# Gate and up of seven groups: heads and rests of the tokens in one product of 512 columns

## The chip, the cores and the metric

The kernel runs on one NeuronCore of a Trainium2 chip. Its time is the device time of one execution in microseconds; runs are told by their median. Profiles and traces are of one profiled execution each, from the hardware profiler.

## The reference

A decoder trunk of two layers for one sequence of 512 tokens with 1,024 features, all in float32. Layer 0 mixes tokens by causal pooling, layer 1 by dilated window attention. Each mixer is followed by a SwiGLU feed-forward layer with 2,816 inner features; each of the four blocks is added to its input behind an RMS norm, and a last norm ends the trunk.

```python
D_FF = -(-8 * D_MODEL // (3 * 256)) * 256          # 2816

def swiglu(h, w_gate, w_up, w_down):
    g = jnp.einsum('bsd,df->bsf', h, w_gate)
    u = jnp.einsum('bsd,df->bsf', h, w_up)
    return jnp.einsum('bsf,fd->bsd', jax.nn.silu(g) * u, w_down)
...
    for i in range(DEPTH):
        h = rmsnorm(x, norm_mix[i])
        ...                                        # y = pool_mixer or attn_mixer of h
        x = x + y
        h = rmsnorm(x, norm_ffn[i])
        x = x + swiglu(h, w_gate[i], w_up[i], w_down[i])
    return rmsnorm(x, norm_final)
```

## The kernel before, in words

**Heads and rests.** The operands of TensorE (PE) are in float32r, a rounded 32-bit type. To keep float32 accuracy, each operand is held as a head ("hi", the value rounded) and a rest ("lo", what rounding took away), and each product is three matmuls into one sum: whi·hi, whi·lo and wlo·hi. A matmul loads a weight block of 128 x 128 and streams 256 or 512 columns through it.

**Weights.** The function `weights` hands out the weights of the next product. They are listed in one queue in the order of use (`enqueue_ffn`); transfers on the queue of SyncE (SP) fill buffers `wraw` and `vraw`, and for sums of two weight blocks a second transfer on GpSimd's queue (POOL) adds the second block while it lands, or VectorE (DVE) adds two buffers (L145). ScalarE (ACT) casts to the head `whi` (L139), DVE subtracts for the rest `wlo` (L143). Both are made up to four products ahead of the one in work.

**Gate and up.** The 2,816 inner features are 22 tiles of 128; a group is two of these, with their gate and up weights, so there are 11 groups. `Group` computes a group's gate and up sums for all tokens as a product of 2 x 2 blocks (feature tile by half of the 1,024 inputs, times that half by half of the tokens) with seven block products instead of eight. Its products i = 0 to 6 go into three PSUM sums: p takes 0, 2, 4 and 6, r takes 1 and 5, q takes 3. Each product (L625) runs over gate and up (g) and four chunks of 128 inputs (c), three matmuls of 256 columns each: 24 matmuls. Its weights are sums or differences of blocks, and its right operand, `RIGHT[i]`, one of seven token blocks: four lie in the normed tokens `h_hi` and `h_lo`, three are differences, in `t_hi` and `t_lo`.

Between the products, `Group.done` moves partial sums on. ACT copies p to `keep` behind product 0 (L636), r to a quarter of `ct` behind product 1 (L638), p to another behind product 2 (L640). DVE adds or subtracts behind products 3 to 5 (L642 to L646). Behind products 5 and 6 ACT applies Silu to the gate quarters (L647, L649, L653), DVE multiplies by up, and `first_half` and `second_half` combine the quarters into the seven left operands `u` of the down product, again as heads and rests (L320 ACT, L321 DVE).

**Down.** For blocks of three groups, `down` does the product with w_down by the same scheme of seven, 18 matmuls of 512 columns for each of two token blocks of 128 x 2 (L712), and DVE adds or subtracts each sum to the residual stream `x` (L719, L721).

**Order.** PE runs in the order in which the program is written: groups 0 and 1 interleaved, groups 2 and 3, down of block 0, groups 4 to 6, down of block 1, groups 7 to 9, down of block 2, group 10, and a last down product for groups 9 and 10 without the scheme. For the other engines a scheduler sorts by priority when the program is built, and the order of an engine's instructions is fixed by then. What runs right behind a product has priority `URGENT`. The kernel uses eight PSUM banks of 512 columns: four are `mm`, and p and r have two buffers each in the feed-forward layer.

## Time and profile before

| | |
|---|---|
| median of three runs | 1000.8 us (1000.61 to 1001.02) |
| the profiled execution | 1000.84 us, span of its instructions 999.0 us |
| granted clock of TensorE | 0.999 |
| busy PE / DVE / ACT / POOL | 990.7 / 784.6 / 529.5 / 113.1 us |
| matmuls | 6575 |
| the chain: gate and up (L625: p, r, mm) | 25%, 13% and 6% of the span |
| the chain: down (L712: r, p, mm) | 10%, 5% and 2% of the span |

The chain of waits follows the work that ended last back from the end: what released each instruction, or the one before it on its engine. Its rows give a start, a length and a name, with the count of instructions that were merged. Rows of groups give line, engine, operation, tile names (out<-in) and shape, then busy time and mean duration in ns, then the engine's idle time ahead of them and what ended it. A matmul's duration reaches into those behind it, so its price in a stream is the distance between starts. A row of windows gives the stretch, its length, then for PE, weight loads, DVE, ACT and POOL the busy time and number of instructions, then the clock and the transfers.

### The profile page before, as it was taken

How to read it: one execution, taken by the hardware profiler on the slowest of the kernel's cores; microseconds unless marked ns; L12 is line 12 of the kernel's file. 1: busy time of each engine (PE TensorE's matmuls, PEld its weight loads, DVE VectorE, ACT ScalarE, POOL GpSimd, SP SyncE). 2: the span in 40 equal slices, each digit the busy share in tenths (PEclk: the TensorE clock that was granted, in tenths of full speed). 3: DMA queues.
4: the chain of work that ended last, by engine and by line, in shares of the span. 5: the costliest groups of instructions: out<-in, count | busy, mean ns of one | idle time of the engine just before them, and what ended most of it. 6: DMA issues, size and time to landing. Idle time of an engine off the chain costs nothing.

```text
span 999.0 us, 16591 instructions
## 1 busy us (share of the span) xinstructions
PE 990.7 (99%) x6575; PEld 908.5 (91%) x6575; DVE 784.6 (79%) x1116; ACT 529.5 (53%) x838; POOL 113.1 (11%) x114
## 2 busy tenths in 40 slices
PE   9999999999999999999999999999999999999997
PEld 8888999989989998989888899899998998999896
DVE  6475799898888888777887557479989889788875
ACT  5573666545644554573543544356654554455354
POOL 0002010110011100002112024101011100111000
PEclk9999999999999999999999999999999999999999
DMA  9457277668559755524211249427666855975522
GB/s 334 177 168 190 60 197 177 151 187 233 149 126 292 182 137 148 183 76 135 83 58 53 62 153 284 92 64 196 174 158 200 234 148 123 289 179 138 155 67 84
DMA packets 76461, 157.29 MB, mean 157 GB/s; under 512 B 5904, under 2 KB 6288, under 8 KB 76384
## 3 DMA queue, kind: packets, MB, share of 16 engines
q1 hardware_dynamic: 58000, 121.00, 36.2%
q0 software_dynamic: 18096, 34.98, 20.3%
q8 instruction: 51, 0.84, 0.3%
q10 hardware_dynamic: 288, 0.27, 0.1%
q14 instruction: 26, 0.21, 0.1%
HBM read 154.08 MB, written 2.13 MB: 156 GB/s over the span
## 4 chain that ended last, share of the span: by engine, by line
PE 97%; ACT 1%; DMA 1%; DVE 1%; POOL 0%; issue 0%; DVEq 0%; ACTq 0%
PE p L625 25%; PE r L625 13%; PE r L712 10%; PE mm L625 6%; PE p L712 5%; PE mm L766 4%; PE mm L227 4%; PE mm L229 4%; PE mm L228 4%; PE mm L712 2%; PE early L443 2%; PE mm L363 2%; PE mm L361 2%; PE mm L362 2%; PE early L490 1%; PE tp L955 1%
## 5 line engine op out<-in xcount | busy, mean ns | idle before, releaser
L139 ACT CAST whi<-wraw 128x1024 fp32r<-128x1024 f32 (+2 forms) x189 | 184.9, 981 | 186.7 <-issue 45.8
L143 DVE TENSOR_TENSOR wlo<-wraw,whi 128x1024 fp32r<-128x1024 f32 (+2 forms) x190 | 221.1, 1165 | 76.2 <-ACT whi L139 75.7
L139 ACT CAST whi<-vraw 128x1024 fp32r<-128x1024 f32 (+1 forms) x102 | 99.6, 977 | 144.8 <-DVE vraw L145 53.7
L625 PE MATMUL p<-t_hi,wlo 128*128 128x256 f32 x528 | 149.8, 284 | 0.0
L625 PE MATMUL p<-t_lo,whi 128*128 128x256 f32 x528 | 149.4, 283 | 0.0
L625 PE MATMUL p<-t_hi,whi 128*128 128x256 f32 x528 | 148.4, 281 | 0.0
L143 DVE TENSOR_TENSOR wlo<-vraw,whi 128x1024 fp32r<-128x1024 f32 (+1 forms) x102 | 114.9, 1127 | 14.0 <-ACT whi L139 13.7
L625 PEld LDWEIGHTS p<-t_hi,whi 128*128 128x128 f32 x528 | 100.0, 189 | 0.0
L625 PE MATMUL r<-h_hi,wlo 128*128 128x256 f32 x352 | 99.9, 284 | 0.0
L625 PEld LDWEIGHTS p<-t_hi,wlo 128*128 128x128 f32 x528 | 99.6, 189 | 0.0
L625 PE MATMUL r<-h_lo,whi 128*128 128x256 f32 x352 | 99.6, 283 | 0.0
L625 PEld LDWEIGHTS p<-t_lo,whi 128*128 128x128 f32 x528 | 99.3, 188 | 0.0
L625 PE MATMUL r<-h_hi,whi 128*128 128x256 f32 x352 | 99.0, 281 | 0.0
L145 DVE TENSOR_TENSOR vraw<-vraw,wraw 128x1024 f32<-128x1024 f32 x68 | 76.6, 1127 | 0.8
L107 POOL DMA_DIRECT2D wraw<-w x22 | 26.7, 1211 | 435.6 <-DVE wlo L143 125.5
L625 PEld LDWEIGHTS r<-h_hi,whi 128*128 128x128 f32 x352 | 66.7, 189 | 0.0
L625 PEld LDWEIGHTS r<-h_hi,wlo 128*128 128x128 f32 x352 | 66.4, 189 | 0.0
L625 PEld LDWEIGHTS r<-h_lo,whi 128*128 128x128 f32 x352 | 66.2, 188 | 0.0
L227 PE MATMUL mm<-h_hi,whi 128*128 128x512 f32 (+1 forms) x176 | 64.8, 368 | 0.0
L229 PE MATMUL mm<-h_hi,wlo 128*128 128x512 f32 (+1 forms) x176 | 63.6, 361 | 0.0
L228 PE MATMUL mm<-h_lo,whi 128*128 128x512 f32 (+1 forms) x176 | 63.5, 361 | 0.0
L712 PE MATMUL r<-whi,u_lo 128*128 128x512 f32 x144 | 56.1, 390 | 0.0
(329 smaller groups left out, 2493.8 us busy)
## 6 DMA issues: line engine op xcount, KB each, us to landing
wraw<-w SPq DMA_DIRECT2D x116, 512.0 KB, 4.7
wraw<-w_down SPq DMA_DIRECT2D x32, 512.0 KB, 3.6
vraw<-w SPq DMA_DIRECT2D x22, 512.0 KB, 5.2
wraw<-w POOLq DMA_DIRECT2D x22, 512.0 KB, 7.6
vraw<-w POOLq DMA_DIRECT2D x22, 512.0 KB, 8.6
wraw<-wT SPq DMA_DIRECT2D x16, 512.0 KB, 4.4
wraw<-w_down SPq DMA_DIRECT2D x24, 256.0 KB, 2.7
vraw<-w_down SPq DMA_DIRECT2D x6, 512.0 KB, 5.5
```

Source lines behind the costliest of these rows:

```text
L107: nc.gpsimd.dma_start(dst, more, accum_op=ALU.add)
L139: nc.scalar.copy(hi[:, :n], raw[:, :n])
L143: nc.vector.tensor_sub(lo[:, :n], raw[:, :n], hi[:, :n].bitcast(F32))
L145: nc.vector.tensor_add(raws[into][:, :n], raws[into][:, :n], raws[more][:, :n])
L227: nc.tensor.matmul(ps, lhsT=whi, rhs=xhi, start=first, stop=False, **kw)
L228: nc.tensor.matmul(ps, lhsT=whi, rhs=xlo, start=False, stop=False, **kw)
L229: nc.tensor.matmul(ps, lhsT=wlo, rhs=xhi, start=False, stop=last, **kw)
L361: nc.tensor.matmul(ps, lhsT=xhi, rhs=w[0][:, k, :], start=first, stop=False)
L362: nc.tensor.matmul(ps, lhsT=xhi, rhs=w[1][:, k, :], start=False, stop=False)
L625: nc.tensor.matmul(ps[:, g, :], lhsT=w[:, g, c, :], rhs=xx[:, c, :], start=i in (0, 1, 3) and g + c + k == 0, stop=c == 3 and k == 2, skip ...
L712: nc.tensor.matmul(acc[t], lhsT=u, rhs=w, start=i in (0, 1, 3) and c + k == 0, stop=c == len(pairs) - 1 and k == 2, skip_group_check=True,)
L766: nc.tensor.matmul(ps, lhsT=u, rhs=w[:, m, :], start=z + m + k == 0, stop=z == 1 and m == 1 and k == 2,)
```

## The change

Groups 3 to 9 ("paired") of each layer get another form of product. The other groups keep theirs.

- Heads and rests of the tokens become one tile (`h`, `t2` to `t4`), so that one matmul can stream both: 256 columns of hi and 256 of lo.
- A paired group's sums are two banks for each of gate and up: four tiles of two banks, two called A (used by turns), one Q and one C, which take all eight. `mm` is closed and opened again around these groups.
- Products 0, 2, 3, 5 and 6 stream hi and lo through whi in one matmul of 512 columns, so that whi·hi and whi·lo lie side by side, and wlo·hi is added to one of the two halves. Products 1 and 4 keep three matmuls of 256.
- 0, 2, 4 and 6 go to A, 3 to Q, 1 and 5 to C. ACT copies A to Q behind product 0 and A to C behind product 2 (1,024 columns each, within PSUM); products 3 and 1 then add on top. When a sum is done, ACT copies one half out and DVE adds the other.
- The order is a list, `PLAN`. A paired group's weights are used in the order 2, 3, 1, 4, then 5 and 6; product 0 of the next group comes ahead of 5 and 6. Down steps are taken apart: the first stands ahead of 5 and 6 of group 3, 6 or 9, the others behind, and product 0 of the next group ahead of the last.
- Down uses the tiles A, C and Q. Its product 0 is copied to Q, onto which product 3 adds, and a sum of both token blocks is added to `x` at once.
- The second half of group 1 is issued behind the copy that moves the first sums of group 2.

```diff
--- before.py
+++ after.py
-FFN_ORDER = (
-    [("two", 0)] + [("quad", n) for n in (2, 3)] + [("down", 0)]
-    + [("quad", n) for n in (4, 5, 6)] + [("down", 1)] + [("quad", n) for n in (7, 8, 9)] + [("down", 2)]
-    + [("quad", 10)] + [("last", 3)]
-)
-TWO = [(g, i) for g in (0, 1) for i in (0, 3)] + [(g, i) for i in (1, 2, 4, 5, 6) for g in (0, 1)]
+TWO = [("one", g, i) for g in (0, 1) for i in (0, 3)] + [("one", g, i) for i in (1, 2, 4, 5, 6) for g in (0, 1)]
+BODY, USED = (1, 2, 3, 4), (2, 3, 1, 4)
+PAIRED = range(3, 10)
+def _plan():
+    first = lambda n: [("quad", n, 0)] if n in PAIRED else []
+    steps = TWO + [("one", 2, i) for i in range(6)] + first(3) + [("one", 2, 6)]
+    for n in PAIRED:
+        steps += [("quad", n, i) for i in USED]
+        ends = [("quad", n, 5), ("quad", n, 6)]
+        if n % 3 == 0:
+            b = n // 3 - 1
+            steps += [("down", b, 0)] + ends + [("down", b, i) for i in range(1, 6)] + first(n + 1) + [("down", b, 6)]
+        else:
+            steps += first(n + 1) + ends
+    return steps + [("one", 10, i) for i in range(7)] + [("last", 3, 0)]
+PLAN = _plan()
...
-    mm = ctx.enter_context(tc.tile_pool(name="mm", bufs=4, space=bass.MemoryType.PSUM))
+    class Banks:
+        def open(self):
+            self.held = ExitStack()
+            self.pool = self.held.enter_context(tc.tile_pool(name="mm", bufs=4, space=bass.MemoryType.PSUM, reuse_waits="tile"))
+        def close(self):
+            self.held.close()
+        def tile(self, *_, **__):
+            return self.pool.tile([P, S], F32, name="mm")
+    mm = Banks()
+    mm.open()
...
+        for kind, n, i in PLAN:
+            if kind == "one":
+                quad(n, i, 5 if n < 2 else 10)
+            elif kind == "quad":
+                if i == USED[0]:
+                    for each in BODY:
+                        quad(n, each)
...
-    h_both = [stat.tile([P, NC * S + 2 * SHIFT], F32R, name=f"h_{part}") for part in ("hi", "lo")]
+    h_both = stat.tile([P, 2, NC * S + 2 * SHIFT], F32R, name="h")
+    def tokens_both(shift):
+        return h_both[:, :, shift : shift + NC * S].rearrange("p z (c s) -> p z c s", c=NC)
...
+            blocks = lambda k, n: h_z[:, :, 4 * k : 4 * k + 4, HALVES[n]]
...
-            t2, t3, t4 = ([fp.tile([P, 4, 256], F32R, name=f"t_{part}{i}") for part in ("hi", "lo")] for i in (2, 3, 4))
+            t_both = [fp.tile([P, 4, 2, 256], F32R, name=f"t{i}").rearrange("p k z c -> p z k c") for i in (2, 3, 4)]
...
+            RIGHT = [blocks(0, 0), blocks(0, 1), t_both[0], blocks(1, 0), t_both[1], blocks(1, 1), t_both[2]]
...
+                def product(self, i, held=0):
+                    whi, wlo = weights(gu[self.n][i], held=held)
+                    right = RIGHT[i]
+                    if self.pairs:
+                        a, q, c = self.pairs
+                        to = (a, c, a, q, a, c, a)[i]
+                        places = [(g, k) for g in range(2) for k in range(4)]
+                        mat = lambda o, w, m, **kw: nc.tensor.matmul(o, lhsT=w, rhs=m, skip_group_check=True, **kw)
+                        own = lambda g: to[:, g, HALVES[i == 1]]
+                        if i in (1, 4):
+                            for g, k in places:
+                                mat(own(g), whi[:, g, k, :], right[:, 0, k, :], start=False, stop=False)
+                                mat(own(g), whi[:, g, k, :], right[:, 1, k, :], start=False, stop=False)
+                                mat(own(g), wlo[:, g, k, :], right[:, 0, k, :], start=False, stop=k == 3)
+                        else:
+                            for g, k in places:
+                                both = to[:, g, :].rearrange("p (z c) -> p z c", z=2)
+                                mat(both, whi[:, g, k, :], right[:, :, k, :], start=i == 0 and k == 0, stop=False)
+                            for g, k in places:
+                                mat(own(g), wlo[:, g, k, :], right[:, 0, k, :], start=False, stop=k == 3)
+                        with tc.high_priority(URGENT if i < 5 else 100):
+                            self.paired_done(i)
+                        return
...
+                def paired_done(self, i):
+                    ct = self.ct
+                    a, q, c = self.pairs
+                    own, more = HALVES
+                    if i == 0:
+                        nc.scalar.copy(q, a)
+                    elif i == 2:
+                        nc.scalar.copy(c, a)
+                    elif i == 3:
+                        nc.scalar.copy(ct[:, 0, 0], q[:, :, more])
+                        nc.vector.tensor_add(ct[:, 0, 0], q[:, :, own], ct[:, 0, 0])
+                    elif i == 1:
+                        nc.scalar.copy(ct[:, 1, 1], c[:, :, more])
+                    elif i == 4:
+                        nc.vector.scalar_tensor_tensor(
+                            ct[:, 1, 1], a[:, :, own], -1.0, ct[:, 1, 1], op0=ALU.mult, op1=ALU.subtract
+                        )
+                    elif i == 5:
+                        nc.scalar.copy(ct[:, 0, 1], c[:, :, more])
+                        nc.vector.tensor_add(ct[:, 0, 1], c[:, :, own], ct[:, 0, 1])
+                        self.gate_first()
+                    elif i == 6:
+                        nc.scalar.copy(ct[:, 1, 0], a[:, :, more])
+                        nc.vector.scalar_tensor_tensor(
+                            ct[:, 1, 0], a[:, :, own], -1.0, ct[:, 1, 0], op0=ALU.mult, op1=ALU.subtract
+                        )
+                        nc.scalar.activation(ct[:, 1, 0, 0, :], ct[:, 1, 0, 0, :], AF.Silu)
+                        nc.vector.tensor_mul(ct[:, 1, 0, 0, :], ct[:, 1, 0, 0, :], ct[:, 1, 0, 1, :])
+                        self.second_half()
...
-                        self.second_half()
+                        if self.n != 1:
+                            self.second_half()
...
+            class Down:
+                def __init__(self, b, p, r, q):
+                    self.b, self.accs, self.p, self.q = b, (p, r, p, q, p, r, p), p, q
+                def product(self, i):
+                    pairs, js = BLOCKS[self.b], dn[self.b]
+                    where = (0, 1, 2, 3, 6, 5, 4)
+                    target = ((0, 0, 1), (1, 1, -1), (0, 1, 1), (0, 0, 1), (1, 1, -1), (0, 1, 1), (1, 0, -1))
+                    ws = [weights(j[i], held=z) for z, j in enumerate(js)]
                     half, n, sign = target[i]
+                    acc = self.accs[i]
...
-                                    acc[t], lhsT=u, rhs=w, start=i in (0, 1, 3) and c + k == 0,
+                                    acc[:, t, :], lhsT=u, rhs=w, start=i in (0, 1) and c + k == 0,
...
+                    with tc.high_priority(URGENT):
+                        to = x[:, 2 * n : 2 * n + 2, COLS[half]]
+                        if i == 0:
+                            nc.scalar.copy(self.q, acc)
+                        elif sign > 0:
+                            nc.vector.tensor_add(to, acc, to)
+                        else:
+                            nc.vector.tensor_sub(to, to, acc)
...
+                if kind == "quad" and i == 0:
+                    groups[n] = Group(n, ct_common, (A[0], Q, C))
+                    A.reverse()
...
+                groups[n].product(i, held={1: -2, 2: 1, 3: 1}.get(i, 0) if kind == "quad" else 0)
+                if (n, i) == (2, 0):
+                    with tc.high_priority(100), tc.issue_after(groups[2].kept.ins):
+                        groups[1].second_half()
...
+                if (n, i) == (1, 6):
+                    fps.close()
+                    mm.close()
+                    fps.open("ffpairs", [P, 2, S], 1)
+                    *A, Q, C = (fps.tile(f"pair{i}") for i in range(4))
+                    A.reverse()
```

PE, a group's products 0 and 1, before (`p` and `r` are their sums):

```order
L625 MATMUL p<-h_hi,whi 128x256
L625 MATMUL p<-h_lo,whi 128x256
L625 MATMUL p<-h_hi,wlo 128x256
L625 MATMUL r<-h_hi,whi 128x256
L625 MATMUL r<-h_lo,whi 128x256
L625 MATMUL r<-h_hi,wlo 128x256
```

PE, products 2, 3 and the begin of 1 of group 3 in the change (`pair_1539` is A, `pair_1540` Q, `pair_1541` C, `t_1000` a token difference):

```order
L668 MATMUL pair_1539<-t_1000,whi 128x512 x8
L668 MATMUL pair_1539<-t_1000,wlo 128x256 x8
L668 MATMUL pair_1540<-h,whi 128x512 x8
L668 MATMUL pair_1540<-h,wlo 128x256 x8
L668 MATMUL pair_1541<-h,whi 128x256 x2
L668 MATMUL pair_1541<-h,wlo 128x256
```

Where 24 matmuls of 256 columns alternated in threes, eight of 512 stand together and then eight of 256; product 1 keeps its threes.

ACT, from the end of group 4 into group 5, before:

```order
L653 ACTIVATE ct<-p 128x256
L320 CAST u_hi<-ct 128x512
L139 CAST whi<-vraw 128x1024
L636 COPY keep<-p 128x512
L320 CAST u_hi<-ct 128x1280
L139 CAST whi<-wraw 128x1024
L638 COPY ct<-r 128x512
```

The same place in the change (`pair_1538` and `pair_1539` are the two A):

```order
L706 COPY pair_1540<-pair_1538 128x1024
L166 CAST whi<-wraw 128x1024
L719 COPY ct<-pair_1541 128x512
L166 CAST whi<-wraw 128x1024
L733 ACTIVATE ct<-ct 128x2x256
L723 COPY ct<-pair_1539 128x512
L166 CAST whi<-vraw 128x1024
L727 ACTIVATE ct<-ct 128x256
L708 COPY pair_1541<-pair_1538 128x1024
L351 CAST u_hi<-ct 128x512
```

The copy of A to Q (L706) stands ahead of the evacuations of products 5 and 6 (L719, L723), and the copy of A to C (L708) behind product 6's evacuation, a cast of a summed weight and a Silu.

ACT around the begin of group 2, before:

```order
L653 ACTIVATE ct_second<-p 128x256
L636 COPY keep<-p 128x512
L139 CAST whi<-vraw 128x1024
L139 CAST whi<-wraw 128x1024
L638 COPY ct<-r 128x512
L320 CAST u_hi<-ct_second 128x1280
```

And in the change (`pair_1538` holds the sums p of group 2, `pair_1541` its r):

```order
L756 ACTIVATE ct_second<-p 128x256
L166 CAST whi<-vraw 128x1024
L743 COPY keep<-pair_1538 128x512
L351 CAST u_hi<-ct_second 128x1280
L166 CAST whi<-wraw 128x1024
L745 COPY ct<-pair_1541 128x512
```

The copy to `keep` has a weight cast ahead of it now, and the cast of group 1's second half (1,280 columns) follows that copy instead of the one behind product 1.

More of the change, by code (lines that the diff above doesn't have):

```diff
@@ L635, in done @@
                     if i == 0:
-                        nc.scalar.copy(keep, p)
+                        self.kept = nc.scalar.copy(keep, p)
                     elif i == 1:
@@ new lines, in ffn @@
+            groups = {0: Group(0, ct_common), 1: Group(1, ct_tile(hn, "ct_second"))}
+            downs = {}
+            with tc.issue_after(third_chain):
+                first_tokens(0, t1r)
+                first_tokens(1, b21r)
+            for at, (kind, n, i) in enumerate(PLAN[:-1]):
+                if at in (0, 2):
+                    b = 2 + at // 2
+                    if b == 2:
+                        late_banks[b] = third
+                        norm.prepare(3, COLS)
+                    else:
+                        late_banks[b] = [r_tile(), by_four(mm.tile())]
+                        for half in range(2):
+                            norm.turn(b, half, late_banks[b][half])
+                    late(b, 1)
+                if at in (4, 6, 8):
+                    for b in (2, 3):
+                        late(b, at // 2)
+                if kind == "down":
+                    if i == 0:
+                        downs[n] = Down(n, A[0], C, Q)
+                        A.reverse()
+                    downs[n].product(i)
+                    continue
+                if kind == "quad" and i == 0:
+                    groups[n] = Group(n, ct_common, (A[0], Q, C))
+                    A.reverse()
+                elif i == 0 and n not in groups:
+                    if n == 10:
+                        fps.close()
+                        mm.open()
+                        fps.open("ffps", [P, S], 2)
+                    groups[n] = Group(n, ct_common)
+                groups[n].product(i, held={1: -2, 2: 1, 3: 1}.get(i, 0) if kind == "quad" else 0)
+                if (n, i) == (2, 0):
+                    with tc.high_priority(100), tc.issue_after(groups[2].kept.ins):
+                        groups[1].second_half()
```

129 lines of the change are left out of this document (48 added, 81 removed).

## The prediction

> **What bounds the kernel now.** I read the page's busy shares, the waits of PE, then the chain of waits.
>
> ```profile
> PE 990.7 (99%) x6575; PEld 908.5 (91%) x6575; DVE 784.6 (79%) x1116; ACT 529.5 (53%) x838; POOL 113.1 (11%) x114
> PE 97%; ACT 1%; DMA 1%; DVE 1%; POOL 0%; issue 0%; DVEq 0%; ACTq 0%
> PE mm L261 <- DVE odd_rows L255: 1.1, 1, 1.1
> PE mm L1129 <- DVE v L1135: 0.5, 1, 0.5
> PE mm L1129 <- ACT ropea L1115: 0.3, 1, 0.3
> core 0: 999.0 us, clock 0.999
> ```
>
> A busy PE need not be a PE that has no gaps, but the three rows of its waits are all that there are, 1.9 us in 999.0, none in a feed-forward layer, and the granted clock is full. So PE's own stream of matmuls sets the time, and what counts is the distance from one matmul's start to the next's. A matmul's duration (0.28 us) does not tell that, since matmuls overlap; the chain does, as it merges runs without a gap:
>
> ```profile
> 173.16 5.70 PE p L625 x48
> 224.54 2.88 PE p L625 x24
> 241.82 5.76 PE p L625 x48
> 285.02 4.12 PE r L712 x18
> 289.14 4.08 PE p L712 x18
> ```
>
> L625 is gate and up with 256 columns: 5.76 / 48 = 120.0 ns each. In each layer's groups 0 to 3, ahead of the first down step, it is 5.70 / 48 = 118.7 ns. L712 is down with 512 columns: 4.08 / 18 = 226.7 ns. Twice the columns cost 106.7 ns more, not 120: a matmul has a price of 13.3 ns that does not grow with its columns.
>
> **The change, part by part.**
>
> *Fewer matmuls.* In groups 3 to 9 of both layers (14 groups), five of seven products replace whi·hi and whi·lo (two of 256 columns) by one of 512, for 2 x 4 weight blocks each: 14 x 5 x 8 = 560 matmuls fewer, with their weight loads; column counts are the same. In groups 4 to 9, 480 merges at 2 x 120.0 − 226.7 = 13.3 ns give 6.4 us. In group 3, 80 merges at 2 x 118.7 − 226.7 = 10.7 ns give 0.9 us. Behind a layer's first 512-wide products the 256-wide ones stand at 120.0, so I expect group 3's other 88 to slip from 118.7 to 120.0: 2 x 88 x 1.3 ns = 0.2 us back. Sum −7.0 us; a bound is 560 x 13.3 = 7.5.
>
> The Trainium skill ("TensorE: Matmul & The Clock Gate", section "Back-to-back issue gap") gives N / 2.4 + 2.5 ns as the gap of a warm matmul. Its slope is the trace's (106.7 ns for 256 columns), its fixed part is not (13.3 here); by the page's figure the merges would be worth, as an estimate, 560 x 2.5 ns = 1.4 us.
>
> *More switches from 256 to 512 columns.* Such a switch has a price of its own at present in most places:
>
> ```profile
> 284.85 0.39 PE L712 MATMUL r<-whi,u_hi 128*128 128x512 f32 x1
> ...
> 286.71 0.39 PE L712 MATMUL r<-whi,u_lo 128*128 128x512 f32 x1
> 743.46 0.39 PE L712 MATMUL r<-whi,u_hi 128*128 128x512 f32 x1
> ...
> 745.28 0.39 PE L712 MATMUL r<-whi,u_lo 128*128 128x512 f32 x1
> ```
>
> Each pair is the first and the ninth 512-wide matmul after a run of 256-wide ones: eight spacings in 1.86 us at 285 (232 ns each, 0.04 over the steady 1.81), in 1.82 at 743 (nothing extra). The change makes 78 switches of 12, as a paired product is eight of 512 and then eight of 256. 66 x 0.04 = 2.6 us is one bound, nothing the other. The dear row stands behind 168 matmuls of 256 columns, four of five new switches behind only eight, so I take a quarter: +0.7 us. If it is a lasting state that each such run brings back, 2.6.
>
> *ACT gets the copies.* Of a paired group, sums move by two ACT copies of 1,024 columns within PSUM and four of 512, where there were three of 512; on DVE the last quarter needs one subtraction of 512 columns more.
>
> ```profile
> L638 ACT COPY ct<-r 128x512 f32<-128x512 f32 x20 | 11.7, 583 | 5.9 <-DVE u_lo L321 5.9
> L139 ACT CAST whi<-wraw 128x1024 fp32r<-128x1024 f32 x156 | 163.6, 1051 | 130.8 <-issue 32.3 <-PE p L625 20.5 <-PE mm L228 17.8
> L283 ACT ACTIVATE p<-x 128x512 f32<-128x512 f32 x15 | 9.0, 603 | 14.1 <-DVE x L349 10.9 <-DVE r L302 1.8 <-DVE ss L285 1.4
> L283 ACT ACTIVATE odd_rows<-x 128x512 f32<-128x512 f32 x12 | 7.5, 626 | 4.3 <-DVE x L349 4.3
> 244.70:264.86 20.16, 20.16 (x170) 20.16 (x170) 17.18 (x21) 11.99 (x16) 2.08 (x2) 1.00 0.59 145
> 227.45 0.59 ACT L636 COPY keep<-p 128x512 f32<-128x512 f32 x1 [0.24 <-PE p L625]
> L649 ACT ACTIVATE ct<-ct 128x256 f32<-128x256 f32 x20 | 8.2, 412 | 0.0
> L719 DVE TENSOR_TENSOR x<-r,x 128x512 f32<-128x512 f32 x24 | 16.5, 686 | 0.0
> L145 DVE TENSOR_TENSOR vraw<-vraw,wraw 128x1024 f32<-128x1024 f32 x56 | 68.3, 1220 | 0.6
> ```
>
> No row copies from PSUM to PSUM. The squares write 512 columns to PSUM in 603 ns and to SBUF in 626, so the target is no penalty; 1,024 columns lie between one cast of that size (1.05 us) and two copies (2 x 0.583 = 1.17). I take 1.1. Group 5 is a window of 20.16 us, in which DVE is busy 17.18 and ACT 11.99 (the third and fourth pairs of the row). ACT gets 2 x 1.1 + 0.58, about 2.8 us more, DVE 0.7. Both still fit into the 19.6 us that a group will take, but DVE at some 91% can run late.
>
> Where PE could meet a copy: C has one buffer. The copy from A to C starts when product 2 ends (the keep row shows 0.03 us between the last matmul's slot, 224.54 + 2.88 in the chain, and the copy), and product 1 needs it. Only product 3 lies between: 8 x 226.7 + 8 x 120.0 ns = 2.77 us. Less 0.03 and 1.17 it leaves 1.57 us for what ACT has queued ahead. In the new order that is the rest of the group before (a copy 0.58, DVE's subtraction 0.69, Silu 0.41) and one cast (1.05): 2.73 us of work, released when product 6 ends, 2.77 us before product 2 does. So ACT is about free when the copy is due. Cost 0, with 1.5 us to spare. Queued behind that copy on ACT are a cast of u and casts of weights that are made up to four products ahead; at 2.8 us a product, a wait of 1 us there does not reach PE. The copy from A to Q has two products to be done in, and A alternates between two.
>
> *Down.* Product 0's sums reach the output through Q (an ACT copy, then PE adds product 3 to them), so an addition to x goes; the others are done for both token blocks at once. The same 756 matmuls at 226.7. DVE saves: per down step 14 additions of 0.69 (9.6 us) become six of 1,024 columns, 1.22 each (7.3). Its first product into C waits for group 3's last use of C with product 6 between, 2.77 us against a copy and an addition, 0.58 + 0.69. Cost 0.
>
> *The late cast.* In group 2, the copy that frees the first sums now stands behind one cast of a summed weight:
>
> ```profile
> 158.96 0.59 ACT L636 COPY keep<-p 128x512 f32<-128x512 f32 x1
> 160.27 1.06 ACT L139 CAST whi<-vraw 128x1024 fp32r<-128x1024 f32 x1 [0.72 <-DVE vraw L145]
> 161.77 2.85 PE p L625 x24
> ```
>
> Today the copy ends at 159.55, 2.2 us ahead of the product that overwrites the sums (161.77). Behind that cast it would end near 160.27 + 1.06 + 0.59 = 161.92. So PE's cover there is gone: between 0 and 0.3 us in each layer; I take 0.1 in all. The second layer has the same steps. The 1,280-wide cast of group 1 follows the copy in both kernels.
>
> *Transfers.* Loads, their queues (SP, and POOL's accumulating ones) and their sizes stay; weights are used in the order 2, 3, 1, 4 within a group, split ahead in the old order. They follow freed buffers, that is PE, which is 3% faster in these groups. Cost 0.
>
> Sum: −7.0 + 0.7 + 0.1 = −6.2 us. The profiled execution took 1000.84 us itself, 0.04 over the median, 1.8 of it outside its span: **994.6 us**, and as median the same.
>
> **Rivals.**
>
> A. *The switches cost their full price*, 0.04 us x 66: −7.0 + 2.6 + 0.1 = −4.3, **996.5 us**. For it: with 285.02 above, the first product of a down step is dear in five of six places:
>
> ```profile
> 195.95 4.11 PE r L712 x18
> ...
> 374.10 4.12 PE r L712 x18
> 743.62 4.08 PE r L712 x18
> ...
> 832.66 4.12 PE r L712 x18
> ...
> 921.74 4.12 PE r L712 x18
> ```
>
> Against it: the row at 743, and only eight matmuls between.
>
> B. *Slower: ACT is held ahead of the copy to C by a cast that waits for DVE.* The order of ACT's instructions is fixed when the program is built, and casts of summed weights wait for DVE's sums:
>
> ```profile
> ACT whi L139 <- DVE vraw L145: 53.7, 26, 2.8
> ```
>
> 26 such waits today, 53.7 us, the longest 2.8, and harmless, as nothing behind them is due. In the new order such a cast stands in most groups one to three places ahead of that copy. If it starts 2.8 us after product 2's end, the copy is late by 2.8 + 1.05 − 1.57 = 2.3 us; in 14 groups that is 32 us, at half of them 16: −6.2 + 16 = +10, **1011 us**. The kernel is slower from 6.2 / 14 = 0.44 us a group. Against it: the sums that these casts wait for hang on transfers and on DVE, not on product 2, so such a wait starts well before the copy is due, and DVE has 9% to spare.
>
> C. *The merged form does not run at 226.7*, so the change does not do what it says. Its right operand is two runs of 256 columns, for h in two halves of one tile, where L712 reads one run. If a run, not a matmul, has the 13.3 ns, 560 merges give nothing: **1000.9 us** with the 0.1 above. Against it, from the attention stage, where L227 to L229 read 256 columns in four runs of 64:
>
> ```profile
> 449.82 0.28 PE L228 MATMUL mm<-h_lo,whi 128*128 128x256 f32 x1
> 449.94 0.28 PE L229 MATMUL mm<-h_hi,wlo 128*128 128x256 f32 x1
> 450.06 0.28 PE L227 MATMUL mm<-h_hi,whi 128*128 128x256 f32 x1
> ```
>
> 120 ns apart, as with one run. A weaker form has a small fixed price and the rest of the 13.3 in what stays; it would end between 994.6 and 1000.9; the two spacings speak against it, as their difference is what the columns take and the rest is 13.3 in both. By the Trainium skill's page named above it would be 999.4, as an estimate.
>
> **How the numbers follow.** Forecast 0.64 (994.6, its own bounds 993.3 with all merges at 13.3 and free switches, and 995.7 with half the switches' price and 0.3 us of waits in each layer's group 2); A 0.16; several short waits of PE at the thin places, 0.2 to 0.3 us a group, so near 998, 0.08; B 0.06; C with its weaker form 0.06. The range 993.1 to 998.2 leaves out B, C and little else. What a measurement can tell from no change is 0.2%, 2.0 us. Faster takes the first three cases, 0.88; same C, 0.06; slower B, 0.06.
>
> **What would show it.** In the chain, a paired product as 8 + 8 matmuls in 2.77 to 2.81 us where 24 took 2.88, and a group from product to product in 19.6 us, not 20.16. PE's matmuls 560 fewer, with 0.04 us a product more if A holds. PE's waits still without a line of the feed-forward layers; a wait of a product into C for ACT is B, and a wait in group 2 for the copy of its first sums is the thin place. Spacings near 240 ns in the 512-wide merged matmuls would make C right and the prediction wrong, a row of 2.10 or more us for ACT's copies in PSUM would undo the cover that I claim.

## The result and the profile after

The changed kernel takes 995.83 us (median of six runs, 995.1 to 996.37) against 1001.0 for the kernel before in the same comparison: a ratio of 0.9948, with a 95% interval of 0.9935 to 0.9962. The profiled execution took 995.85 us, its span 994.1 (before: 999.0). Forecast were 994.6 us and a range of 993.1 to 998.2. So it is faster, by 5.2 us where a gain of 6.2 was forecast.

In the changed kernel L668 is gate and up of the paired groups, L694 that of the others, L818 down, L706 the copy from A to Q, L708 that from A to C. The page's first part and its line on the chain of waits, after:

```profile
PE 985.3 (99%) x6015; PEld 878.0 (88%) x6015; DVE 782.2 (79%) x1082; ACT 562.5 (57%) x886; POOL 113.2 (11%) x114
PE 97%; ACT 1%; DMA 1%; DVE 1%; POOL 0%; issue 0%; DVEq 0%; ACTq 0%
```

560 matmuls fewer, as counted; ACT is up 33 us, and nothing but PE sets the end. The waits of PE, all of them:

```profile
PE mm L292 <- DVE odd_rows L286: 1.1, 1, 1.1
PE mm L1255 <- DVE v L1261: 0.9, 1, 0.9
PE mm L1255 <- ACT ropea L1241: 0.3, 1, 0.3
```

Still no line of a feed-forward layer. The second has grown from 0.5 to 0.9 us; it lies in the attention stage, which the change leaves alone. So where 1 us of the forecast gain went must be read from the distances of the matmuls. The chain after, layer 0, from group 3's first product to the end of group 5 (start, length, name, count):

```profile
172.70 2.82 PE pair L668 x16
175.52 2.88 PE pair L694 x24
178.40 11.32 PE pair L668 x80
189.72 4.13 PE pair L818 x18
193.84 5.61 PE pair L668 x32
199.45 20.41 PE pair L818 x90
...
226.81 50.79 PE pair L668 x336
```

"Merged" are the 512-wide matmuls of the paired products, "narrow" those of 256 columns. A paired product of 8 + 8 takes 2.80 to 2.82 us where 24 narrow ones took 2.88, but the sum of the forecast had 2.77. The parts of one product, behind a matmul of down, on the timeline:

```profile
193.45 0.39 PE L818 MATMUL pair<-whi,u_lo 128*128 128x512 f32 x1
193.68 2.02 PE L668 MATMUL pair<-h,whi 128*128 128x512 f32 x8
195.54 0.64 PE L668 MATMUL pair<-h,wlo 128*128 128x256 f32 x4
```

Eight merged matmuls take 195.54 − 193.68 = 1.86 us, 232 ns each, and this run stands behind 18 matmuls of down, with no narrow one between. Means over all starts of the traces (ns from one start to the next, and in brackets their sum in us):

| | merged, 512 | narrow, paired groups | narrow, other groups | down, 512 |
|---|---|---|---|---|
| before | – | 119.8 (281.8) | 119.2 (160.3) | 226.9 (171.6) |
| the change | 232.5 (130.2) | 118.7 (146.2) | 119.4 (160.5) | 227.4 (171.9) |

The sums fall from 613.6 to 608.8, 4.8 us, which is nearly all of the span's 4.9. The 1,120 narrow matmuls that went took 1,120 x 119.8 ns = 134.2 us, the 560 merged ones that came take 130.2: a gain of 4.0 us. The 1,232 narrow ones that are left in the paired groups take 1.4 us less than before (147.6 to 146.2). Those of the other groups take 0.3 more, and down takes 0.3 more.

### The profile page after: what moved, and what is told of

Read it like the earlier page. It is cut to its first block, busy times and chain, and to the rows that moved or that the text cites. A ratio compares the mean times of both kernels' runs of the same rounds, so it can differ in the third digit from the quotient of the medians.

```text
span 994.1 us, 15515 instructions
## 1 busy us (share of the span) xinstructions
PE 985.3 (99%) x6015; PEld 878.0 (88%) x6015; DVE 782.2 (79%) x1082; ACT 562.5 (57%) x886; POOL 113.2 (11%) x114
## 4 chain that ended last, share of the span: by engine, by line
PE 97%; ACT 1%; DMA 1%; DVE 1%; POOL 0%; issue 0%; DVEq 0%; ACTq 0%
PE pair L668 28%; PE pair L818 17%; PE p L694 7%; PE mm L891 4%; PE mm L254 4%; PE mm L256 4%; PE mm L255 4%; PE pair L694 4%; PE r L694 3%; PE early L474 2%; PE mm L392 2%; PE mm L394 2%; PE mm L393 2%; PE mm L694 2%; PE early L521 1%; PE tp L1081 1%
## 5 line engine op out<-in xcount | busy, mean ns | idle before, releaser
L668 PE MATMUL pair<-h,whi 128*128 128x512 f32 (+1 forms) x560 | 125.5, 349 | 0.0
L668 PEld LDWEIGHTS pair<-h,whi 128*128 128x128 f32 x560 | 95.4, 188 | 11.8
L818 PE MATMUL pair<-whi,u_lo 128*128 128x512 f32 x252 | 98.3, 390 | 0.0
L818 PE MATMUL pair<-wlo,u_hi 128*128 128x512 f32 x252 | 98.2, 390 | 0.0
L818 PE MATMUL pair<-whi,u_hi 128*128 128x512 f32 x252 | 98.1, 389 | 0.0
L668 PE MATMUL pair<-t,whi 128*128 128x512 f32 (+1 forms) x448 | 97.2, 338 | 0.0
L668 PEld LDWEIGHTS pair<-t,whi 128*128 128x128 f32 x448 | 74.8, 188 | 7.7
L668 PE MATMUL pair<-h,wlo 128*128 128x256 f32 x448 | 78.2, 281 | 0.0
L668 PEld LDWEIGHTS pair<-h,wlo 128*128 128x128 f32 x448 | 66.8, 188 | 3.9
L254 PE MATMUL mm<-h,whi 128*128 128x512 f32 (+1 forms) x176 | 64.8, 368 | 0.0
L255 PE MATMUL mm<-h,whi 128*128 128x512 f32 (+1 forms) x176 | 63.5, 361 | 0.0
L668 PE MATMUL pair<-t,wlo 128*128 128x256 f32 x336 | 62.6, 281 | 0.0
L818 PEld LDWEIGHTS pair<-whi,u_lo 128*128 128x128 f32 x252 | 47.3, 188 | 10.0
L818 PEld LDWEIGHTS pair<-wlo,u_hi 128*128 128x128 f32 x252 | 47.3, 188 | 9.5
L818 PEld LDWEIGHTS pair<-whi,u_hi 128*128 128x128 f32 x252 | 47.3, 188 | 9.4
```

The costliest lines, as they stand in the source:

```text
L254: nc.tensor.matmul(ps, lhsT=whi, rhs=xhi, start=first, stop=False, **kw)
L255: nc.tensor.matmul(ps, lhsT=whi, rhs=xlo, start=False, stop=False, **kw)
L668: mat = lambda o, w, m, **kw: nc.tensor.matmul(o, lhsT=w, rhs=m, skip_group_check=True, **kw)
L818: nc.tensor.matmul(acc[:, t, :], lhsT=u, rhs=w, start=i in (0, 1) and c + k == 0, stop=c == len(pairs) - 1 and k == 2, skip_group_check=True,)
```

## The experiments

First theory (S): a switch from 256 to 512 columns is dear, and the merged matmuls, always eight behind a switch, never get past it. The first rival (F): something about the merged matmuls keeps them at 232.4 ns, however many stand in a row. The row at 193.68 speaks for F. In all diffs the loops are those of `product` in the changed kernel, unless said otherwise.

**Longer runs.**

Two functions, `heads` and `rests`, hold the two loops of a merged product, and some products call them the other way round.

```diff
...
+                            late = {0: (6, 2), 1: (5,), 2: (5, 2)}[self.n % 3]
+                            for part in (rests, heads) if i in late else (heads, rests):
+                                part()
```

> Some paired products do their eight rests first and then their eight merged matmuls, so that the merged ones of neighbouring products join: 24 runs of 512-wide matmuls per layer where the change has 36, seven of them 16 long and none of the instructions removed. Theory S (a switch from 256 to 512 columns has a price: the first eight or nine 512-wide matmuls behind it stand at 232.4 ns, later ones at 226.7): 24 switches fewer at 8 x 5.7 ns give 1.1 us, so 994.7 us, and the ninth to sixteenth merged matmul of a joined run stand at 226.7 ns. Rival F (PE has two states, one with 226.7 and 120.0 ns for 512 and 256 columns, one with 232.4 and 118.7, and the paired products hold it in the second whatever stands ahead of them): 995.8 us as in the change, and every merged matmul at 232.4 ns.

996.54 us (ratio to before 0.9956, 0.9942 to 0.9969): not better than the change. The chain's stretch of groups 4 and 5:

```profile
227.35 50.84 PE pair L668 x336
```

50.84 us where the change has 50.79. Merged matmuls stand at 232.7 ns on average, also in the second half of a run of 16. S falls with this: more merged matmuls in a row do not bring 226.7.

**One by one.**

```diff
                                 mat(both, whi[:, g, k, :], right[:, :, k, :], start=i == 0 and k == 0, stop=False)
-                            for g, k in places:
                                 mat(own(g), wlo[:, g, k, :], right[:, 0, k, :], start=False, stop=k == 3)
```

> Merged matmul and rest alternate one by one (512, 256, 512, 256 ...) in the five products instead of eight and eight; the same instructions. Theory S: every merged matmul stands within the first nine behind a switch, so all 560 at 232.4 ns and the time is that of the change, 995.8 us; if instead one switch costs its 45 ns whole each time, some 490 switches more cost 22 us, 1018 us. Rival F: 232.4 and 118.7 ns, 995.8 us.

996.25 us (0.9961, 0.9947 to 0.9975). 490 switches more cost 0.4 us or nothing. The means are 230.6 and 119.9 ns, in sum the change's: 350.5 for a pair against 351.2.

**Runs of 80.**

```diff
-                                mat(own(g), wlo[:, g, k, :], right[:, 0, k, :], start=False, stop=k == 3)
+                            for w in (whi, wlo):
...
+                                    mat(both, w[:, g, k, :], right[:, :, k, :], ...)
```

> The rests of the weights stream heads and rests of the tokens too (wlo times lo is added, which the reference's precision does not need): 560 matmuls of 256 columns become 512 wide, so that five products in a row are 80 matmuls of 512 columns without a 256-wide one between. Theory S: nearly all 1,120 at 226.7 ns from the tenth of a run on, the 256-wide ones behind such a run at 120.0: 995.8 + 560 x (226.7 - 118.7) ns - 560 x 5.7 ns + 672 x 1.3 ns = 995.8 + 60.5 - 3.2 + 0.9, near 1054 us. Rival F: all 1,120 at 232.4 ns: 995.8 + 560 x (232.4 - 118.7) ns, near 1059.5 us.

1059.63 us (one run), F's number to 0.1 us. One of the long runs, first, second and last eight:

```profile
245.29 2.02 PE L668 MATMUL pair<-h,whi 128*128 128x512 f32 x8
247.15 2.02 PE L668 MATMUL pair<-h,wlo 128*128 128x512 f32 x8
...
262.02 2.02 PE L668 MATMUL pair<-h,wlo 128*128 128x512 f32 x8
263.88 0.40 PE L668 MATMUL pair<-h,whi 128*128 128x256 f32 x2
```

80 matmuls in 18.59 us, 232.4 ns each, and the last eight (1.86 us) are no faster than the first. That rules S out for runs of 80 as well.

**The structure without the merging.**

```diff
-                                mat(both, whi[:, g, k, :], right[:, :, k, :], ...)
+                                for w, z, at in ((whi, 0, 0), (whi, 1, 1), (wlo, 0, 0)):
+                                    mat(to[:, g, HALVES[at]], w[:, g, k, :], right[:, z, k, :], ...)
```

> The change's tiles, order, copies and evacuations, but the merged matmul is taken apart again: whi times hi into one half, whi times lo into the other, wlo times hi, 256 columns each, in the old order, so 560 matmuls more than the change. If the gain is the merging alone: 1000.9 us with the 256-wide ones at 120.0 ns behind the first down step as before; if they stand at 118.7 ns there, 12 groups x 168 x 1.3 ns = 2.6 us less, 998.3 us. If the order, the copies or the late cast carry gain or loss of their own, the time differs from both at unchanged spacings: a wait of PE that is gone or new would show it.

1001.64 us, ratio to before 1.0007 (0.9998 to 1.0015): tiles, order, copies and the late cast together are not told from nothing. The narrow ones stand at 120.0 ns behind the first down step, as before (432 in 51.84 us):

```profile
227.08 51.84 PE pair L668 x432
```

So the whole gain, 1001.64 − 995.83 = 5.8 us within this structure, comes with the merging. By the distances, 4.1 us of it are the merged matmuls themselves (1,120 x 119.9 ns = 134.3 us against 130.2), and 1.5 us the other 1,232 narrow ones, which stand at 119.9 ns here and at 118.7 beside merged ones.

**What holds the merged ones at 232.4?** The next theory (W) took what they share with their neighbours: down and the attention stage use each operand twice in most cases, a merged matmul has two new ones.

```diff
-                        places = [(g, k) for g in range(2) for k in range(4)]
+                        places = [(g, k) for k in range(4) for g in range(2)]
```

> In the five merged products the chunk of inputs is the outer loop and gate and up the inner one, so that every second matmul streams the same right operand as the one ahead of it; the same instructions as the change. Theory W (what keeps PE at 226.7 ns for 512 columns is that most matmuls share one operand with the one ahead, as in down, where two of three do; in the change each merged matmul has a new weight block and a new right operand): merged matmuls at 226.7 ns, 560 x 5.7 = 3.2 us less, and the 1,232 narrow ones behind them at 120.0 instead of 118.7, 1.6 us more: 994.2 us. Rival F (merged matmuls hold PE in the state of 232.4 and 118.7 ns whatever their order): 995.8 us, 232.4 ns.

995.79 us (0.9947, 0.9933 to 0.9962), 232.5 ns: no change. And from the other side, in `Down.product`:

```diff
-                        for c, pair in enumerate(pairs):
...
-                            for k, (u, w) in enumerate(((hi, whi), (hi, wlo), (lo, whi))):
+                        for k in range(3):
+                            for c, pair in enumerate(pairs):
```

> In the down product the three forms (head with head, head with rest, rest with head) become the outer loop and the pairs of a block the inner one, so that no matmul shares an operand with the one ahead of it; the same instructions as the change, gate and up as in the change. Theory W: down's 756 matmuls go from 227.4 to 232.4 ns, 3.8 us more, 999.6 us. Rival F: down stays at 227 ns, 995.8 us.

995.84 us (0.9948, 0.9933 to 0.9964); down stays at 227.4 ns without any sharing. W falls.

**Probes.** The places where a merged product stands right behind down's steady stream let one kernel ask seven questions.

```diff
+                            probe = {(3, 5): ..., (4, 0): ..., (4, 2): ..., (6, 5): ..., (7, 0): ..., (7, 2): ..., (9, 5): ...}
-                                mat(both, whi[:, g, k, :], right[:, :, k, :], ...)
+                                w, m = probe(g, k)
+                                mat(out, w, m, ...)
```

> A probe in seven places where a merged product follows straight behind down's steady stream (226.7 ns), so that its eight 512-wide matmuls tell at once whether they keep that distance; in the change all of them stand at 232.2 to 232.4 ns from the first on. These products compute something else (other operands in the eight merged matmuls), all else is as in the change. Group 3, product 5: 512 heads of one row of tokens instead of 256 heads and 256 rests. Group 4, product 0: each weight block used twice in a row. Group 4, product 2: one weight block for all eight. Group 6, product 5: 512 heads, and each weight block twice in a row. Group 7, product 0: the same 512 heads for all eight. Group 7, product 2: the same heads and rests for all eight. Group 9, product 5: tokens as the left operand and 512 columns of weights streamed, as in down. Theory D (heads and rests in one matmul are dear): 226.7 ns in groups 3, 6, 7 (product 0) and 9, 232.4 elsewhere. Theory W2 (a new weight block for each matmul is dear): 226.7 ns in group 4, in group 6 and, if tokens are free of it, in group 9, 232.4 elsewhere. Theory R (weights as the left operand of a 512-wide matmul are dear behind down): 226.7 ns in group 9 alone. If the state has another cause: all seven at 232.4 ns. The time moves by less than 1 us in each case.

996.11 us (one run), and none of the three: 232.2 ns in the first six places, 232.6 in group 9. Not heads beside rests, not the operand's two runs, not new weights. All seven had one thing left in common, tokens (h or t) as one of the operands: streamed in six, loaded as the left operand in group 9. The second set has probes without them.

```diff
+                            u_left = lambda k: u_of[self.n - 1][0][:, k, 0:P]
+                            (6, 5): lambda: [(u_left(k), cols(0), 0) for k in (0, 1)] * 4,
+                            (7, 0): lambda: [(u_left(k), cols(g), g) for g in range(2) for k in (0, 1, 0, 1)],
+                            (7, 2): lambda: plain * 4,
+                            ...
```

> More probes in the seven places behind down's steady stream; these products compute something else, all else is as in the change. Group 3, product 5: all eight merged matmuls into one bank instead of four and four. Group 4, product 0: one matmul eight times, same weights, same tokens, same bank. Group 4, product 2: head and rest of the weights by turns, both 512 wide, the same tokens twice in a row, one bank. Group 6, product 5: left operands from u and 512 columns of weights streamed, as down has them, one bank. Group 7, product 0: the same, four and four into two banks. Group 7, product 2: the merged matmuls four times over, 32 in a row. Group 9, product 5: one matmul with 512 heads 32 times, one bank. The 48 matmuls more in each layer cost 21.8 us, so near 1017.6 us in all cases. Theory K (the change of bank after four matmuls is what costs): 226.7 ns in groups 3, 4, 6 and 9, 232 in the two probes of group 7. Theory U (what is streamed and loaded must be as in down): 226.7 in group 6 and group 7's product 0 alone. Theory L (any new stream needs some nine matmuls to settle, and the state that follows depends on the operands): all at 232 for the first eight, and of the two long ones group 9's at 226.7 from about the tenth on. If none of it decides: 232 ns in all, over their whole length.

1019.49 us (one run), 1.9 over the expected 1017.6; the 512-wide matmuls of the paired groups take 22.2 us more, 0.4 over the expected 21.8, and the trace has longer waits in the two mixers. The distances show theory U's pattern, in both layers. Group 6's probe with u and weights, and the 32 of group 7 with t and weights:

```profile
282.08 1.98 PE L668 MATMUL pair<-whi,u_hi 128*128 128x512 f32 x8
283.89 1.12 PE L668 MATMUL pair<-h,wlo 128*128 128x256 f32 x8
...
315.01 7.62 PE L668 MATMUL pair<-t,whi 128*128 128x512 f32 x32
322.47 0.52 PE L668 MATMUL pair<-t,wlo 128*128 128x256 f32 x3
```

1.81 / 8 = 226 ns against 7.46 / 32 = 233 ns; one bank or two, the same matmul 32 times or 32 different ones, made no difference (group 9's 32 stand at 233.1 too).

**Where the tokens lie.** What sets h and t of these layers apart is their place. The constant `SHIFT`, 32 floats, and a gap tile put them 128 bytes from where they would lie, in both kernels; so streams begin 128 or 384 bytes past a multiple of 512. Weights and u begin at 0 or 256, as do the tokens of the attention stage, whose 512-wide matmuls settle at 226.7 ns. Two runs move the tokens alone: the second gap tile is dropped or resized, and a fixed size for `h` stands in the cut line, so that every other tile keeps its address.

```diff
-SHIFT = 32
+SHIFT = 64
...
-            fp.tile([P, SHIFT], F32, name="gap3")
```

> The tokens of gate and up (h, t) lie 256 bytes from their tiles' begin in SBUF instead of 128 (a constant of 64 floats instead of 32; all else keeps its address). In the change, the streamed tokens of all merged matmuls start at 128 or 384 bytes past a multiple of 512, and the weights at 0; every 512-wide matmul of the kernel that settles at 226.7 ns (attention, down) reads streamed and loaded operands that both start at 0 or 256. Theory A (this place sets the spacing): merged matmuls at 226.7 ns (560 x 5.8 = 3.2 us less), narrow ones at 120.0 (1,232 x 1.3 = 1.6 us more in paired products, 1,344 x 0.6 = 0.8 more in unpaired ones), down without its dear first nine (756 x 0.7 = 0.5 less): 995.8 - 1.3 = 994.5 us. If the place is nothing: 995.8 us and 232.4 ns.

995.88 us (0.9946, 0.9934 to 0.9959), so the time did not move, but the distances did. Behind down (in this kernel merged is L667, down L817):

```profile
195.01 1.98 PE L667 MATMUL pair<-h,whi 128*128 128x512 f32 x8
196.82 1.12 PE L667 MATMUL pair<-h,wlo 128*128 128x256 f32 x8
```

Eight in 1.81 us, 226.6 each, as theory A says, where the change has 1.86. But behind eight narrow ones they stand at 230.1, so with this place a switch does have a price (8 x 3.5 = 28 ns); the mean is 229.4. Narrow ones go to 119.6 in paired groups and 120.2 in the others. The sums: 128.5 + 147.3 + 161.6 + 171.8 = 609.2 us against 608.8. The place matters, and the forecast of the time was wrong mostly by the switches: 560 x 2.7 ns = 1.5 us.

```diff
-SHIFT = 32
+SHIFT = 16
...
-            fp.tile([P, SHIFT], F32, name="gap3")
+            fp.tile([P, 64 - SHIFT], F32, name="gap3")
```

> The same with 64 bytes (16 floats): streamed tokens start at 64 or 320 past a multiple of 512. Theory A in its simple form (multiples of 256 bytes or not): 232.4 and 118.7 ns as with 128 bytes, 995.8 us. If each step away from a multiple of 256 or 128 has a spacing of its own, merged and narrow ones stand at other values, and the time tells whether 128 bytes was the better place for this mix. If the place is nothing: 995.8 us.

**989.7 us**, a ratio to before of 0.988 (0.9865 to 0.9895), 6.1 us under the change: neither number of theory A, and the best kernel of this study. Groups 4 and 5 in the chain, and eight narrow matmuls ahead of the next line on the timeline:

```profile
226.82 49.89 PE pair L668 x336
```

```profile
250.75 1.07 PE L668 MATMUL pair<-h,wlo 128*128 128x256 f32 x8
251.66 0.39 PE L668 MATMUL pair<-h,whi 128*128 128x256 f32 x2
```

49.89 us instead of 50.79. All kinds get closer: merged 229.5 ns (128.5 us), narrow in paired groups 116.3 (143.3), with runs at 113 to 114 like the 0.91 us for eight above, narrow in the others 118.4 (159.2), down 227.3 (171.8). The sum is 602.8, 6.0 under the change's, and the span fell by 5.9 (994.1 to 988.2). How the bytes set the distance stays open; that the tokens' place sets it is shown, as nothing else was moved. What 64 bytes would do for the kernel before was not tried, so it is not shown that the change keeps its lead there.

**The cover of the copy to C.** Rival B hung on the time between the end of the copy from A to C and product 1, for which the prediction gave 1.5 us.

```diff
-                        nc.scalar.copy(c, a)
+                        for _ in range(3):
+                            nc.scalar.copy(c, a)
```

> The copy from A to C is made three times in a row instead of once, in all 14 paired groups, 2.0 us more of ACT's work ahead of product 1. The profile of the change shows between the end of that copy and product 1's first matmul 0.85 us in four groups, 1.22 in four, 1.49 in four and 1.60 in two. If that is the whole cover and PE waits for what is over: 4 x 1.15 + 4 x 0.78 + 4 x 0.51 + 2 x 0.40 = 10.5 us more, 1006.3 us, with a wait of PE for ACT's copy at product 1 in each group. If the cover were the 1.5 us that the prediction worked out, 14 x 0.5 = 7 us more, 1002.8 us. If PE does not wait for that copy at all, 995.8 us.

1040.8 us (1.0403, 1.0381 to 1.0425), 45 us more. Each copy took the forecast 1.0 us, but ACT's order put casts of u between them, which I had not counted:

```profile
280.78 1.01 ACT L709 COPY pair<-pair 128x1024 f32<-128x1024 f32 x1
281.73 0.62 ACT L351 CAST u_hi<-ct 128x512 fp32r<-128x512 f32 x1
282.24 1.01 ACT L709 COPY pair<-pair 128x1024 f32<-128x1024 f32 x1
283.19 1.25 ACT L351 CAST u_hi<-ct 128x1280 fp32r<-128x1280 f32 x1
284.34 1.01 ACT L709 COPY pair<-pair 128x1024 f32<-128x1024 f32 x1
```

So the waits sum to more than 10.5 us, and the time lost is more than the waits. The row of PE's waits, and windows around one of them (the number behind the five pairs is the granted clock):

```profile
PE pair L668 <- ACT pair L709: 27.3, 14, 2.1
```

```profile
284.00:286.40 2.40, 1.00 (x8) 1.00 (x9) 1.93 (x2) 2.40 (x4) 0.00 (x0) 1.00 0.00 0
286.40:289.80 3.40, 3.40 (x18) 3.40 (x17) 1.41 (x2) 0.41 (x1) 0.00 (x0) 0.50 0.18 38
289.80:292.60 2.80, 2.80 (x26) 2.80 (x26) 1.23 (x1) 1.53 (x2) 0.57 (x1) 1.00 0.37 141
```

Behind this wait the clock is granted at half for 3.4 us, and narrow matmuls stand 213 ns apart. By the starts in the trace that follows nine of the 14 waits, 140 matmuls in all; behind the other five there is none of it, though they are as long. The trace's records of the granted clock show when it happens: the nine stretches are 3.413 us each, and the distances between their starts are whole multiples of 3.413 us (51.2, 23.9, 23.9, 51.2 us and so on). Laid on that grid, the nine waits lie whole within one step, and a stretch begins at the step's end; the other five reach across a border between two steps, one of them by 0.07 us only. Why a border has this effect is not shown. L668's distances sum to 321.1 us against 276.4 in the change: 44.7 more, 27.3 of it the waits, 140 x 94 ns = 13.2 us the half rate, and the rest lies in the matmuls next to the waits.

One copy more shows the short waits:

```diff
+                        for _ in range(2):
+                            nc.scalar.copy(c, a)
```

> The copy from A to C is made twice instead of once. By the order of ACT the second copy follows straight behind the first in four groups, behind a cast of 512 columns in eight and behind one of 1,280 in two; its end is then 0.95, 1.46 and 2.1 us later than the first one's. Against the cover of 0.85 us (four groups), 1.22 and 1.49 (four each) and 1.60 (two) that is a wait of PE of 0.1, 0.24, 0 and 0.5 us: 2.4 us in all. If short waits cost what they last: 995.8 + 2.4 = 998.2 us. If each wait, however short, brings the stretch of half rate that followed the 2 us waits of the run with two more copies (17.8 us in 14 waits, 1.3 us each), ten waits give 13 us more, near 1011 us, and the granted clock of the span drops under 0.999. The prediction's rival B was slower than before from 0.44 us of lateness a group, at no price but the wait itself.

1000.44 us (0.9997, 0.9987 to 1.0006): 4.6 us more, and all of the change's gain is gone. The granted clock of the span stays at 0.999, so waits of this length bring no half rate. They show mostly as waits of the weight load:

```profile
PEld pair L668 <- ACT pair L709: 3.6, 10, 0.6
```

Ten waits, in the ten groups that the expectation named. From the starts in the trace, the matmul ahead of the wait stands 0.24 to 0.54 us longer than 0.119, 3.2 us in sum, and the next one 0.10 us longer, 1.0 in sum: a short wait costs its length and 0.1 us to start again. The expectation was 0.14 us a wait too low in the four groups of the thinnest cover, 0.05 in the others, and had not the 0.1 us.

## Why the prediction was right, and what was wrong in it

*What bounds the kernel.* Right. PE's stream sets the time before and after, and the sums of the distances account for 4.8 of 4.9 us.

*Fewer matmuls, −7.0 us.* The count (560) is right; the step that failed is the 226.7 ns for a merged matmul, taken from down's rows. It is 232.5, so the merges brought 4.0 us where the sum had 6.4 + 0.9. A row of the same columns was not enough: its operands lie elsewhere, and the runs with the tokens moved show that the distance follows the place. Some of the miss came back, by luck, from a step that was wrong as well: I expected group 3's narrow matmuls to slip from 118.7 to 120.0 behind 512-wide ones (0.2 us lost), but in the change the narrow ones of the paired groups stand at 118.7 on average, and the 1,232 that are left there gained 1.4 us. Without that, the time would have been about 997.2 us, still in the range but on the far side of rival A's.

*The switches, +0.7 us, and rival A.* The sum of these two terms was −6.3; the measured one is −5.1 (−4.0 − 1.4 + 0.3 for down). Rival A's 996.5 is nearer to 995.83 than my 994.6, and the forecast's own upper bound, 995.7, was missed by 0.1. But for the merged matmuls A's mechanism falls: with the tokens at 128 bytes a merged matmul takes 232 ns first or last, in runs of 8, 16 or 80. The dear row at 285 belongs to down's operands: there PE takes some nine 512-wide matmuls to settle; with the merged ones' operands it does not settle at all.

*ACT's copies, cost 0.* Right, with less to spare than said. The copies took 1.00 us where I took 1.1 (of 1.05 to 1.17):

```profile
L708 ACT COPY pair<-pair 128x1024 f32<-128x1024 f32 x14 | 14.1, 1004 | 0.6 <-PE pair L668 0.6
L706 ACT COPY pair<-pair 128x1024 f32<-128x1024 f32 x14 | 14.0, 1002 | 9.8 <-PE pair L668 9.8
```

The cover was 0.85 us in four of 14 groups, not 1.5. There, behind a down step, a cast that waits for DVE's sum holds the copy, as rival B had it, only by less:

```profile
229.45 1.05 ACT L166 CAST whi<-vraw 128x1024 fp32r<-128x1024 f32 x1 [1.24 <-DVE vraw L172]
230.40 1.01 ACT L708 COPY pair<-pair 128x1024 f32<-128x1024 f32 x1
```

Product 2 ended at 229.62, so the copy is 0.78 us late, and ends at 231.41, 0.85 ahead of product 1 at 232.26. Group 5's window shows why nothing worse came: DVE stayed at 89%, ACT at 70%.

```profile
237.96:257.70 19.74, 19.74 (x131) 17.96 (x129) 17.61 (x22) 13.84 (x18) 2.74 (x3) 1.00 0.82 199
```

The group takes 19.74 us, not the 19.6 forecast, as the merged matmuls take longer. Rival B's point, 0.44 us a group, was about right: the gain was gone at 4.6 / 14 = 0.33 us a group.

*Down, cost 0; transfers, cost 0.* No wait of PE names them. But down cost 0.3 us: its mean rose from 226.9 to 227.4 ns, as its stream is begun 16 times instead of six. In ten of the 16 starts the first nine matmuls stand at 232 ns and take some 46 ns more than nine settled ones, in the other six 12 ns. Four of the ten stand behind only eight narrow matmuls (the first at 222.52). So for down the price that rival A put on a switch is real, and the prediction had put it at nothing there.

*The late cast, +0.1.* Right in kind, and low: 0.2 us. The copy ran at 160.37, later than before, and ended at 160.95; the first weights of the product that overwrites its sums were loaded at 161.01:

```profile
159.42 1.06 ACT L166 CAST whi<-vraw 128x1024 fp32r<-128x1024 f32 x1 [0.96 <-DVE vraw L172]
160.37 0.58 ACT L743 COPY keep<-pair 128x512 f32<-128x512 f32 x1
160.79 0.19 PEld L694 LDWEIGHTS pair<-h,wlo 128*128 128x128 f32 x1
161.01 0.30 PEld L694 LDWEIGHTS pair<-t,whi 128*128 128x128 f32 x2
161.23 0.19 PEld L694 LDWEIGHTS pair<-t,wlo 128*128 128x128 f32 x1
```

Loads stand 0.12 us apart in this stream, so that one came 0.1 us late, behind the copy, and the matmul of 161.02 stands 206 ns from the next one; in the second layer, at 706.73, it is 199 ns. With two smaller ones of 146 and 153 ns behind a later copy (L747, at 166.81 and 712.51) the four are 0.23 us over 119 ns each. The trace before has none of them, and they are most of the 0.3 us that the other groups took more. The rows of PE's waits are too coarse to show them. The cast started 0.85 us earlier than in the trace before, and still the 2.2 us of cover are gone.

*Rival C.* Half right by accident: the merged form does not run at 226.7 ns. Its reason falls: t streams as one run of 512, h as two of 256, and their merged matmuls stand at 232.5 and 232.4. The Trainium skill ("TensorE: Matmul & The Clock Gate", section "Back-to-back issue gap") stood behind a result of 999.4; the trace disagrees with its fixed part of 2.5 ns, since 512 and 256 columns here take 19 and 12 ns more than N / 2.4.

## What to carry to other kernels

A matmul's price in a stream belongs to its operands' places as well as to its columns: before pricing a new form by a row of the trace, check that the row's operands begin at the same offsets, and try a few offsets of the streamed tile once the kernel is bound by PE (here 64 bytes in place of 128 brought 6.1 us, and the change 5.2). When PE is full, a short wait costs its length and 0.1 us here, and waits of 2 us cost two thirds more than their length (44.7 us for 27.3), so a cover of less than 1 us behind a copy is worth writing down group by group.

## What had not been expected of the hardware

- The place of the streamed tokens in SBUF alone moves a kernel's time by 0.6%: with 64, 128 and 256 bytes the merged matmuls stand at 229.5, 232.5 and 229.4 ns, the narrow ones of the paired groups at 116.3, 118.7 and 119.6, and the time is 989.7, 995.83 and 995.88 us. Single runs of narrow ones reach 113.2 ns.
- Matmuls of one form have more than one steady distance at a full granted clock: in the kernel before, narrow ones with operands at the same offsets stand at 118.7 ns ahead of a layer's first down step (groups 2 and 3) and at 120.0 behind it. What decides it is not shown.
- Of 14 waits of PE of about 2 us, nine were followed by some 15 narrow matmuls at half rate (3.4 us at a granted clock of 0.50 in the window shown), of ten waits of up to 0.54 us none. The Trainium skill ("TensorE: Matmul & The Clock Gate", section "What's actually happening") has the half rate and the 3.4 us, and the trace agrees with both; it asks for an idle window of about 3.4 us first, and here 2.0 us were enough. Whether a stretch followed went with the wait's place on a grid of 3.413 us, as told above.
